# The expert stage of a two-block kernel: weights split by whole units in rings of their own, the further slots' rows on 128 partitions, down products 512 columns wide

## The chip, the cores and the metric

The kernel runs on one core of one Trainium2 chip. The metric is the device time of one execution in microseconds: the median of three runs is 2816.87 us (2815.18 to 2824.26).

## The reference

The program is two transformer blocks on 512 tokens of 1024 features, batch 1, in float32. The first block has two layers, each with a mixer of four kinds (HGRN2, GLA, RWKV7, RetNet, 256 features each) and a feed-forward part; the feed-forward part of its second layer is a mixture of experts. The second block (gated feed-forward, a hybrid of a linear recurrence and windowed attention, gated feed-forward) follows. This case is about the mixture of experts:

```python
def _moe(h, router, wg, wu, wd):            # 8 experts, top 2, hidden width 1408
    probs = jax.nn.softmax((hf @ router).astype(F32), axis=-1)
    top_p, top_i = lax.top_k(probs, TOP_K)
    top_p = top_p / jnp.sum(top_p, -1, keepdims=True)
    gates = jnp.sum(jax.nn.one_hot(top_i, N_EXPERTS, dtype=F32) * top_p[..., None], axis=1)
    for e in range(N_EXPERTS):
        out = out + gates[:, e:e + 1] * _swiglu(hf, wg[e], wu[e], wd[e])
```

`_swiglu(h, wg, wu, wd)` is `(silu(h @ wg) * (h @ wu)) @ wd`.

## The kernel before

**Precision.** A float32 product is made of three products of a rounded type: each operand is split into a high part (an ACT copy, L352) and a low part (a DVE subtraction of the high part, L353), and high x high, high x low and low x high are summed in PSUM. In the expert stage the weights are split on the chip, block by block, as they arrive.

**Routing.** `Moe.route` gives every expert CAP = 160 slots: 128, and CR = 32 further ones. The first expert's inputs are made by products with the slots' places. For the other experts `scatter` writes each token's row to its two slots in DRAM (`xg`) and the gates to `gg`, by indirect DMAs on POOL's queue, while the first expert runs. A token that finds no slot is computed in a branch, `moe_overflow`, at the end of the stage.

**One expert** (`Moe.experts`, once for each of 8) has 33 units of weights, each [128, 1024] float32, 512 KB, loaded on SP's queue:

- gate and up: 11 hidden blocks, each with a gate and an up unit. A unit holds 8 weight blocks of 128 x 128; a block takes two products: high weights against 320 columns (160 slots, high and low part side by side; L1857) and low weights against 160 columns (L1859, the last of a unit L1856). A copy (L1861) and a sum (L1862) take the result from its bank; the silu (L1869), a product of the 32 further slots on POOL (L1871, `rest`) and one of the 128 slots on DVE (L1872) follow, and the hidden rows are split (`hid`).
- down (`moe_down`): 11 units of 128 hidden rows x 1024 columns. The 128 slots are the stationary side; three products in each of four pieces of 256 columns (L2008 to L2010). The 32 further slots are multiplied in plain float32 with the unsplit weights, after every second unit (L2005); the four products of two hidden blocks use four column groups of the array.
- `moe_store` scales the result by the gates and writes it to `yg` in DRAM, on SP's queue.

**Weights.** `Stream` loads a unit into a ring of WR = 3 raw tiles (L661; the down units into a ring of WD = 4), and splits it in four pieces of 256 columns into a ring of WB = 10 pairs of pieces, 2.5 units. A raw tile is free again when its pieces are split and, in down, when L2005 has read it; a piece when its products are done.

**Inputs of the next expert** (`Moe.inputs`). At the last hidden block but one of an expert, SP is asked for the next expert's rows: 128 rows and 32 rows of 1024 columns. After the down blocks in INPUTS (3, 7, 9) PE transposes three, three and two blocks of 128 features, each for both row tiles (L1777); then DVE multiplies by the gain (L1723), POOL adds the bias (L1724), ACT copies the high part (L1725) and POOL subtracts for the low part (L1726).

**Side work.** After each hidden block and each down block, `tick` lets one step of side work go on POOL's queue: scatter in expert 0, clearing in expert 1, the norm's gain and bias on the tokens' rows in expert 2 (eight steps, L1800), the residual's factor in expert 3 (four steps, L1815), gathering the other experts' rows and adding them in expert 7 (L1782, L1826).

**The order of the work.** The order on each engine and queue is fixed when the program is built: a planner goes through the traced instructions in program order, with assumed durations, and lets an instruction go early when its buffers are free. `keep_in_program_order` and `issue_after` pin an instruction behind others of its engine. Queues run strictly in order, SP's too: a load that waits for its buffer holds up what is behind it. The pool of the stage (`me`) waits for all users of the memory that the mixer's pools held before it.

Of the kernel before, what the change touches and what calls it, by code (L numbers as in the profile page):

```python
# [9 lines left out]
F32 = mybir.dt.float32  # L10
# [26 lines left out]
WD = 4  # L37
# [239 lines left out]
def finish(steps):  # L277
    """run a generator, for what it returns"""
# [7 lines left out]
class K:  # L286
# [36 lines left out]
    def warm(self, x, n, bank=None):  # L323
        """keep the tensor engine's clock up over a wait: products of x, at hand, that nothing reads"""
# [37 lines left out]
    def load_x(self, pool, st=None):  # L362
        """the split input, its loads between those of the first weights"""
# [96 lines left out]
    def enter(self, f, hs=slice(0, T)):  # L460
        """block f of the residual, scaled by the next norm's gain: the high part"""
# [17 lines left out]
    def ln_chain(self, tot, sT, g, b, pool, st):  # L479
        """what follows each half of the last output blocks: the norm's input, its statistics, the normed split"""  # L480
# [62 lines left out]
    def resid_in(self, f, sT):  # L543
        """ALPHA times the residual"""
# [68 lines left out]
class Totals:  # L613
    """the Stats' sums per token of the tiles ts, [128 t, len(ts)] each; first() takes what is there before the last blocks"""
# [15 lines left out]
    def first(self):  # L630
        self.add(0)
# [9 lines left out]
class Stream:  # L641
    """the split weights of src, block by block; from unit own on in the pool's own ring"""
# [14 lines left out]
    def load(self, pool=None, bufs=WR):  # L657
        """the next 1024 columns"""
# [31 lines left out]

TWO_PI = 2.0 * math.pi
# [11 lines left out]
INPUTS, PLACES = (3, 7, 9), 9  # L703
# [6 lines left out]
def trig(k, pool):  # L710
    """cosine and sine of the rotary angles, kept in DRAM"""
# [29 lines left out]
class Slots:  # L741
    """a pool whose tiles all share one tag"""
# [1734 lines left out]
```

## Time and profile before

| | |
|---|---|
| median of 3 runs | 2816.87 us (2815.18 to 2824.26) |
| profiled execution, span (first to last instruction) | 2820.5 us |
| mean granted TensorE clock | 0.983 of full speed |
| PE busy | 2716.5 us (96%) |
| DVE busy | 1748.2 us (62%) |
| ACT busy | 1415.1 us (50%) |
| POOL busy | 284.8 us (10%) |
| DMA | 334.07 MB, 118 GB/s on average |
| expert stage, first gate product to last down product | 663.6 us |

PE is the matrix engine's products, PEld its weight loads (they run beside products), DVE, ACT and POOL the vector, scalar and general engines, SP the queue that issues most DMAs. A line such as L353 is a line of the kernel before; L352 and L353 stand for all splits, so the tile names tell which one. Consecutive products overlap in the records, so a product's pitch is read from starts, not from its duration. The granted clock is given as a share of 2.4 GHz.

### The profile page before, as it was taken

How to read it: one execution, taken by the hardware profiler on the slowest of the kernel's cores; microseconds unless marked ns; L12 is line 12 of the kernel's file. 1: busy time of each engine (PE TensorE's matmuls, PEld its weight loads, DVE VectorE, ACT ScalarE, POOL GpSimd, SP SyncE). 2: the span in 40 equal slices, each digit the busy share in tenths (PEclk: the TensorE clock that was granted, in tenths of full speed). 3: DMA queues.
4: the chain of work that ended last, by engine and by line, in shares of the span. 5: the costliest groups of instructions: out<-in, count | busy, mean ns of one | idle time of the engine just before them, and what ended most of it. 6: DMA issues, size and time to landing. Idle time of an engine off the chain costs nothing. (4 is left out here: it accounts for less than half of the span.)

```text
span 2820.5 us, 52447 instructions
## 1 busy us (share of the span) xinstructions
PE 2716.5 (96%) x19484; PEld 2213.6 (78%) x19484; DVE 1748.2 (62%) x4164; ACT 1415.1 (50%) x3561; POOL 284.8 (10%) x362
## 2 busy tenths in 40 slices
PE   8999999999999999998989999889999999999998
PEld 6777688888877776786878888768888877888887
DVE  6664464443476544666998888886554378755543
ACT  5454344333344543465767777664443357544432
POOL 1000120000021000123232111310000010100000
PEclk9999999999999999989999999999999999999999
DMA  4111323322221111168767777733322221232222
GB/s 160 47 46 54 142 67 106 97 98 90 90 85 40 46 61 61 53 221 250 231 224 228 244 249 240 249 99 105 97 97 97 86 74 46 91 99 96 97 96 75
DMA packets 95094, 334.07 MB, mean 118 GB/s; under 512 B 11489, under 2 KB 13953, under 8 KB 94832
## 3 DMA queue, kind: packets, MB, share of 16 engines
q1 hardware_dynamic: 88432, 311.24, 33.7%
q0 software_dynamic: 5824, 18.72, 2.0%
q8 instruction: 156, 2.56, 0.4%
q14 instruction: 106, 0.87, 0.1%
q10 hardware_dynamic: 576, 0.69, 0.1%
HBM read 313.95 MB, written 17.18 MB: 117 GB/s over the span
## 5 line engine op out<-in xcount | busy, mean ns | idle before, releaser
L353 DVE TENSOR_TENSOR wlo<-wraw,whi 128x256 fp32r<-128x256 f32 x2220 | 952.7, 450 | 703.4 <-ACT whi L352 671.4
L352 ACT ACTIVATE whi<-wraw 128x256 fp32r<-128x256 f32 x2220 | 850.2, 411 | 941.6 <-PE bkA L384 760.7
L383 PE MATMUL bkA<-xH,whi 128*128 128x512 f32 x1352 | 542.0, 401 | 2.5 <-DVE sh L916 2.1
L384 PE MATMUL bkA<-xL,whi 128*128 128x512 f32 x1352 | 535.0, 396 | 0.0
L385 PE MATMUL bkA<-xH,wlo 128*128 128x512 f32 x1352 | 533.1, 394 | 0.0
L1857 PE MATMUL bkA<-xe,whi 128*128 128x320 f32 x1408 | 386.2, 351 | 10.9 <-ACT whi L352 10.4
L1859 PE MATMUL bkA<-xe,wlo 128*128 128x160 f32 x1232 | 309.7, 251 | 21.3 <-DVE wlo L353 19.9
L383 PEld LDWEIGHTS bkA<-xH,whi 128*128 128x128 f32 x1352 | 254.9, 189 | 70.8 <-issue 15.2
L384 PEld LDWEIGHTS bkA<-xL,whi 128*128 128x128 f32 x1352 | 255.2, 189 | 59.2 <-issue 10.1
L385 PEld LDWEIGHTS bkA<-xH,wlo 128*128 128x128 f32 x1352 | 255.1, 189 | 56.4 <-issue 4.3
L1857 PEld LDWEIGHTS bkA<-xe,whi 128*128 128x128 f32 x1408 | 262.1, 194 | 15.7 <-ACT whi L352 15.2
L1859 PEld LDWEIGHTS bkA<-xe,wlo 128*128 128x128 f32 x1232 | 241.6, 196 | 40.8 <-DVE wlo L353 38.8
L383 PE MATMUL bkA<-hH,whi 128*128 128x512 f32 (+1 forms) x548 | 207.0, 378 | 0.0
L384 PE MATMUL bkA<-hL,whi 128*128 128x512 f32 (+1 forms) x548 | 206.7, 377 | 0.0
L385 PE MATMUL bkA<-hH,wlo 128*128 128x512 f32 (+1 forms) x548 | 206.5, 377 | 0.0
L385 PEld LDWEIGHTS bkA<-hH,wlo 128*128 128x128 f32 x548 | 102.9, 188 | 21.2
L384 PEld LDWEIGHTS bkA<-hL,whi 128*128 128x128 f32 x548 | 103.0, 188 | 20.9
L383 PEld LDWEIGHTS bkA<-hH,whi 128*128 128x128 f32 x548 | 103.0, 188 | 20.9
L2008 PE MATMUL bkA<-whi,hid 128*128 128x256 f32 x352 | 105.6, 300 | 10.9 <-ACT whi L352 10.9
L2008 PEld LDWEIGHTS bkA<-whi,hid 128*128 128x128 f32 x352 | 67.3, 191 | 52.5 <-ACT whi L352 44.1
L2010 PE MATMUL bkA<-wlo,hid 128*128 128x256 f32 x352 | 100.6, 286 | 3.8 <-DVE wlo L353 3.7
L2009 PE MATMUL bkA<-whi,hid 128*128 128x256 f32 x352 | 99.4, 282 | 0.0
(703 smaller groups left out, 4142.6 us busy)
## 6 DMA issues: line engine op xcount, KB each, us to landing
wraw<-moew SPq DMA_DIRECT2D x264, 512.0 KB, 4.4
wraw<-win SPq DMA_DIRECT2D x76, 512.0 KB, 3.5
wraw<-f0gu SPq DMA_DIRECT2D x44, 512.0 KB, 3.4
wraw<-f1gu SPq DMA_DIRECT2D x44, 512.0 KB, 3.4
wraw<-f2gu SPq DMA_DIRECT2D x44, 512.0 KB, 3.4
wraw<-f0d SPq DMA_DIRECT2D x22, 512.0 KB, 3.5
wraw<-f1d SPq DMA_DIRECT2D x22, 512.0 KB, 3.4
wraw<-f2d SPq DMA_DIRECT2D x22, 512.0 KB, 3.5
```

What stands on the lines that cost most here:

```text
L352: nc.scalar.activation(hi, x, AF.Copy)
L353: nc.vector.tensor_tensor(lo, x, hi.bitcast(F32), op=OP.subtract)
L383: mm(ps, wH, xH, start=first, stop=False)
L384: mm(ps, wH, xL, start=False, stop=False)
L385: mm(ps, wL, xH, start=False, stop=last)
L1857: mm(ps, wH, xf[:, q], start=q == 0, stop=last, skip_group_check=True)
L1859: mm(ps[:, :C], wL, xe[:, q, 0], start=False, stop=False, skip_group_check=True)
L2008: mm(o, hid[:, hb, 0], wH, start=hb == 0 and c * WC % 512 == 0, stop=False, **kw)
L2009: mm(o, hid[:, hb, 1], wH, start=False, stop=False, **kw)
L2010: mm(o, hid[:, hb, 0], wL, start=False, stop=last, **kw)
```

## The change

All in the expert stage:

- A class `MoeStream` replaces `Stream` there. Of every eight units three (`SHARE`) go to the kernel's common ring of 3 raw tiles and five to a ring of MR = 5 of its own; the split parts go to rings of MW = 4 whole units, one ACT copy and one DVE subtraction of 1024 columns each.
- `moe_down` takes the blocks in groups of REST = 4: it fetches and splits the units of the group, then issues the small rows' products of the group, then the products of each block, 512 columns wide.
- `inputs` loads the 32 further rows as four pieces of 256 columns on four times 32 partitions, so all transposes take 128 rows: 4 + 4 for the 128 slots, 2 for the further ones, after blocks 2, 5 and 8. The rows of expert 1 are loaded on POOL's queue, the others on SP's. The four steps behind the transposes (`take_rows`) stay on DVE, POOL, ACT, POOL, for 512, 512 and 256 columns.
- `moe_store` issues on POOL's queue. The side work of experts 2 and 3 is spread over experts 2 to 6, one step in PACE = 8 ticks.
- `hid`, `rest`, `xe`, the row tiles and the store's tiles have one buffer instead of two; the two pools of the stage wait tile by tile for earlier users of their memory. The register load for the overflow branch is placed behind the last weight load on SP.
- Docstrings and comments are dropped.

```diff
-WD = 4
+MR, MW, SHARE = 5, 4, (0, 3, 6)
...
+class MoeStream(Stream):
+    def __init__(self, K_, src, pool):
+        super().__init__(K_, src)
+        self.pool = pool
+    def load(self):
+        k = self.K
+        self.u += 1
+        if self.u % (WR + MR) in SHARE:
+            raw = k.ws.tile([P, 1024], F32, name="wraw", tag="wraw", bufs=WR)
+        else:
+            raw = self.pool.tile([P, 1024], F32, name="mraw", tag="mraw", bufs=MR)
+        self.last = k.nc.sync.dma_start(raw, self.src[self.u])
+        return raw
+    def pieces(self, raw):
+        hi, lo = [self.pool.tile([P, 1024], F32R, name=n, tag=n, bufs=MW) for n in ("mhi", "mlo")]
+        self.K.split(raw, hi, lo)
+        return hi, lo
+    def block(self):
+        if self.j == 8:
+            self.cur, self.j = self.unit(), 0
+        c = slice(self.j * P, self.j * P + P)
+        self.j += 1
+        return [t[:, c] for t in self.cur]
...
-INPUTS, PLACES = (3, 7, 9), 9
+INPUTS, PLACES = (2, 5, 8), 9
+REST, PACE = 4, 8
...
+    def take_rows(self, src, xe, fs, cs, t):
+        nc = self.k.nc
+        g, b = [self.k.par(n)[:, fs] for n in ("ln1g1", "ln1b1")]
+        hi, lo = xe[:, fs, 0, cs], xe[:, fs, 1, cs]
+        n, c = hi.shape[1:]
+        t = t[:, :n * c].rearrange("p (n c) -> p n c", c=c)
...
+            nc.vector.tensor_tensor(t, src, g[:, :, None].to_broadcast([P, n, c]), op=OP.mult)
+        nc.gpsimd.tensor_tensor(t, t, b[:, :, None].to_broadcast([P, n, c]), op=OP.add)
         nc.scalar.activation(hi, t, AF.Copy)
+        return nc.gpsimd.tensor_tensor(lo, t, hi.bitcast(F32), op=OP.subtract)
...
     def inputs(self, e, me):
+        q = nc.gpsimd if e == 1 else nc.sync
+        a, b = me.tile([P, D], F32, name="xra"), me.tile([P, 2 * P], F32, name="xrb")
+        r0 = e * CAP
+        q.dma_start(a, k.xg[r0:r0 + P, :])
+        for n in range(P // CR):
+            q.dma_start(b[n * CR:(n + 1) * CR], k.xg[r0 + P:r0 + CAP, n * 2 * P:(n + 1) * 2 * P])
+        yield
+        xe = me.tile([P, KT, 2, CAP], F32R, name="xe")
         yield xe
+        for src, fs, cs in ((a, slice(0, 4), slice(0, P)), (a, slice(4, KT), slice(0, P)), (b, slice(0, KT), slice(P, CAP))):
+            bank = k.bankB()
+            n = 4 if src is a else 2
+            for f in range(n):
+                c = fs.start * P + f * P
+                nc.tensor.transpose(bank[:, f * P:(f + 1) * P], src[:, c:c + P], k.ident)
...
+            yield self.take_rows(v, xe, fs, cs, me.tile([P, 512], F32, name="ge", tag="ge", bufs=2))
...
-                    yield
+                    yield from range(PACE)
...
-        with tc.tile_pool(name="me", bufs=1) as me:
+        with tc.tile_pool(name="me", bufs=1, reuse_waits="tile") as me, \
+                tc.tile_pool(name="mr", bufs=1, reuse_waits="tile") as mr:
+            ws = MoeStream(k, k.A["moew"], mr)
+            slow = [gains(), residual()]
...
-                        rv = nc.values_load(self.most[0:1, 0:1], min_val=0, max_val=T)
+                        with tc.issue_after(ws.last.ins):
+                            rv = nc.values_load(self.most[0:1, 0:1], min_val=0, max_val=T)
...
+def moe_down(k, ws, hid, rest, side):
+    def fetch():
+        raws.append(ws.raw())
+        cut.append(ws.pieces(raws[-1]))
     for hb in range(NHE):
+        if hb % REST == 0:
+            group = range(hb, min(hb + REST, NHE))
+            for _ in group:
+                fetch()
+            for b in group:
                 for n in range(2):
                     r0 = 32 * (2 * n + b % 2)
                     mm(rb[r0:r0 + CR], rest[:, b], raws[b][:, n * 512:(n + 1) * 512], start=b < 2, stop=b >= NHE - 2, **kw)
+        last = hb == NHE - 1
+        side(hb)
+        wH, wL = cut[hb]
+        for n in range(2):
+            c = slice(n * 512, (n + 1) * 512)
+            mm(yb[n], hid[:, hb, 0], wH[:, c], start=hb == 0, stop=False, **kw)
+            mm(yb[n], hid[:, hb, 1], wH[:, c], start=False, stop=False, **kw)
+            mm(yb[n], hid[:, hb, 0], wL[:, c], start=False, stop=last, **kw)
...
-    nc.sync.dma_start(out[:P], y)
+    nc.gpsimd.dma_start(out[:P], y)
```

## Rows read from the trace of the kernel before

**Rows 1.** The page's first line

```profile
span 2820.5 us, 52447 instructions
```

**Rows 2.** Stretches, per expert: length, busy PE, PEld, DVE, ACT, POOL, clock, DMA, GB/s

```profile
1208.50:1305.70 97.20, 81.69 (x549) 70.14 (x549) 63.19 (x178) 56.98 (x181) 28.77 (x35) 0.91 0.81 242
1305.70:1385.10 79.40, 76.71 (x546) 66.49 (x545) 66.85 (x182) 56.82 (x182) 18.45 (x21) 0.98 0.76 248
1385.10:1470.60 85.50, 75.12 (x547) 66.33 (x546) 81.96 (x183) 57.14 (x183) 29.54 (x25) 0.98 0.67 220
1470.60:1548.80 78.20, 75.91 (x547) 65.22 (x546) 67.73 (x181) 56.12 (x182) 21.45 (x21) 1.00 0.74 241
1548.80:1776.70 227.90, 226.81 (x1635) 195.89 (x1633) 201.95 (x550) 172.24 (x548) 31.66 (x51) 1.00 0.74 243
1776.70:1872.10 95.40, 80.46 (x534) 70.67 (x532) 81.74 (x183) 56.33 (x182) 31.61 (x27) 0.91 0.66 212
```

**Rows 3.** Timeline of PE in gate and up of expert 5 (start, length, line)

```profile
1645.04 0.24 PE L1859 MATMUL bkA<-xe,wlo 128*128 128x160 f32 x1
...
1646.32 0.24 PE L1859 MATMUL bkA<-xe,wlo 128*128 128x160 f32 x1
```

**Rows 4.** Timeline of PE in down of expert 5

```profile
1685.55 0.28 PE L2010 MATMUL bkA<-wlo,hid 128*128 128x256 f32 x1
1685.76 1.07 PE L2005 MATMUL bkB<-wraw,rest 128*32 128x512 f32 x8
1686.76 0.39 PE L2008 MATMUL bkA<-whi,hid 128*128 128x256 f32 x1
...
1687.10 0.28 PE L2010 MATMUL bkA<-wlo,hid 128*128 128x256 f32 x1
...
1689.55 0.28 PE L2010 MATMUL bkA<-wlo,hid 128*128 128x256 f32 x1
1689.66 1.31 PE L1777 MATMUL bkB<-ca,xr 128*128 128x128 f32 x6
1690.91 0.64 PE L2005 MATMUL bkB<-wraw,rest 128*32 128x512 f32 x4
```

**Rows 5.** Waits in the expert stage: total us, times, longest

```profile
PEld bkA L2008 <- ACT whi L352: 44.1, 41, 10.9
...
PEld bkA L1859 <- DVE wlo L353: 38.8, 79, 2.6
```

**Rows 6.** Groups by line, expert stage: busy, mean ns | idle before, releasers

```profile
L353 DVE TENSOR_TENSOR wlo<-wraw,whi 128x256 fp32r<-128x256 f32 x1051 | 467.2, 481 | 82.0 <-ACT whi L352 69.1 <-PE bkA L1859 3.3 <-PE bkA L1857 2.9
...
L352 ACT ACTIVATE whi<-wraw 128x256 fp32r<-128x256 f32 x1053 | 376.0, 406 | 121.1 <-DMA wraw<-moew 87.8 <-PE bkA L1859 10.4 <-PE bkA L1857 7.3
```

**Rows 7.** Stretches: gate scatter, a full one, two with a lower clock

```profile
1264.00:1286.00 22.00, 12.60 (x89) 9.34 (x88) 9.66 (x29) 8.12 (x28) 9.85 (x10) 0.87 1.01 177
1214.00:1218.00 4.00, 4.00 (x33) 4.00 (x32) 2.59 (x9) 3.44 (x12) 0.70 (x2) 1.00 1.03 412
1280.20:1290.40 10.20, 2.94 (x16) 2.71 (x19) 2.51 (x6) 3.37 (x10) 1.49 (x2) 0.50 0.87 244
1396.30:1399.60 3.30, 3.30 (x16) 3.30 (x15) 3.25 (x11) 1.89 (x7) 0.68 (x2) 0.50 0.56 187
```

**Rows 8.** Groups by line and shape: a DVE product 1024 columns wide

```profile
L1301 DVE TENSOR_TENSOR Qp<-Qp,FT 128x1024 f32<-128x1024 f32 x6 | 7.3, 1218 | 2.6 <-ACT FT L1266 2.6
```

**Rows 9.** Timeline of PE before the stage: products of 512 columns

```profile
1167.39 0.39 PE L383 MATMUL bkA<-yH,whi 128*128 128x512 f32 x1
...
1168.79 0.39 PE L383 MATMUL bkA<-yH,whi 128*128 128x512 f32 x1
```

**Rows 10.** Timeline of PE in the routing: 128-row transposes

```profile
1182.38 0.60 PE L1587 MATMUL bkA<-ca,ZR 128*128 128x128 f32 x4
```

**Rows 11.** Timeline of POOL and DVE in expert 2

```profile
1405.18 2.43 POOL L1800 TENSOR_TENSOR hTok<-hTok,lnrow 128x1024 f32<-128x1024 f32 x1
1405.29 2.60 DVE L353 TENSOR_TENSOR wlo<-wraw,whi 128x256 fp32r<-128x256 f32 x1
```

More of the change, by code (lines that the diff above doesn't have):

```diff
@@ L1687, in route @@
                            start=n == 0 and i == 0 and q == 0, stop=i == NT - 1 and q == 1, skip_group_check=True)
-            self.take(b, self.xe0, fs, self.sl.tile([P, 3, C], name="ge"), True)
+            self.take(b, self.xe0, fs, self.sl.tile([P, 3, C], name="ge"))
         V.tensor_reduce(mx, gate, axis=AX.X, op=OP.add)
@@ L1708, in route, with take @@
         V.tensor_copy(self.most, mb[:, P - 1:P])
-    def take(self, bank, xe, fs, t, first=False):
+    def take(self, bank, xe, fs, t):
         nc = self.k.nc
-        V = nc.vector
         f, n = fs[0], len(fs)
@@ L1815, in residual @@
                 nc.gpsimd.tensor_scalar(h[:, i], h[:, i], ALPHA, None, op0=OP.mult)
-                yield
+                yield from range(PACE)
         def collect():
@@ L1835, in places @@
             return cp
-        with tc.tile_pool(name="me", bufs=1) as me:
+        with tc.tile_pool(name="me", bufs=1, reuse_waits="tile") as me, \
+                tc.tile_pool(name="mr", bufs=1, reuse_waits="tile") as mr:
+            ws = MoeStream(k, k.A["moew"], mr)
             nxt = self.xe0
+            slow = [gains(), residual()]
             for e in range(NE):
                 xe = nxt
-                beside = [self.scatter(), self.slot_gates(me)] if e == 0 else [clear()] if e == 1 else [gains()] if e == 2 else [residual()] if e == 3 else [collect()] if e == NE - 1 else []
+                beside = [self.scatter(), self.slot_gates(me)] if e == 0 else [clear()] if e == 1 else [collect()] if e == NE - 1 else slow
                 def tick(after):
@@ L1863, in hidden @@
                     return a
-                hid = me.tile([P, NHE, 2, P], F32R, name="hid", tag="hid", bufs=2)
-                rest = me.tile([P, NHE, CR], F32, name="rest", tag="rest", bufs=2)
+                hid = me.tile([P, NHE, 2, P], F32R, name="hid")
+                rest = me.tile([P, NHE, CR], F32, name="rest")
                 for hb in range(NHE):
@@ L1876, in experts @@
                         step = self.inputs(e + 1, me)
-                        nxt = next(step)
+                        next(step)
+                if e + 1 < NE:
+                    nxt = next(step)
                 def side(hb):
@@ L1890, in experts @@
                 at, after = [], [last]
-                yb, rb = moe_down(k, ws, hid, rest, me, side)
+                yb, rb = moe_down(k, ws, hid, rest, side)
                 gs = [self.gs[:, n, e:e + 1] for n in range(2)]
@@ L1985, in combine @@
                 scale(i - 2)
-def moe_down(k, ws, hid, rest, pool, side):
+def moe_down(k, ws, hid, rest, side):
     nc = k.nc
@@ L1994, in moe_down @@
     kw = dict(skip_group_check=True)
-    raws = []
+    raws, cut = [], []
+    def fetch():
+        raws.append(ws.raw())
+        cut.append(ws.pieces(raws[-1]))
     for hb in range(NHE):
-        raws.append(ws.raw(pool, WD))
-        last = hb == NHE - 1
-        pieces = ws.pieces(raws[hb])
-        side(hb)
-        if hb % 2 or last:
-            for b in range(hb - hb % 2, hb + 1):
+        if hb % REST == 0:
[3 more added lines that the diff above has]
+            for b in group:
                 for n in range(2):
@@ L2005, in moe_down @@
                     mm(rb[r0:r0 + CR], rest[:, b], raws[b][:, n * 512:(n + 1) * 512], start=b < 2, stop=b >= NHE - 2, **kw)
-        for c, (wH, wL) in enumerate(pieces):
-            o = yb[c * WC // 512][:, c * WC % 512:c * WC % 512 + WC]
-            mm(o, hid[:, hb, 0], wH, start=hb == 0 and c * WC % 512 == 0, stop=False, **kw)
-            mm(o, hid[:, hb, 1], wH, start=False, stop=False, **kw)
-            mm(o, hid[:, hb, 0], wL, start=False, stop=last, **kw)
+        last = hb == NHE - 1
[6 more added lines that the diff above has]
+            mm(yb[n], hid[:, hb, 0], wL[:, c], start=False, stop=last, **kw)
     return yb, rb
@@ L2015, in moe_store @@
     nc = k.nc
-    y = pool.tile([P, D], F32, name="yr", tag="yr", bufs=2)
-    r = pool.tile([P, 512], F32, name="yq", tag="yq", bufs=2)
+    y = pool.tile([P, D], F32, name="yr")
+    r = pool.tile([P, 512], F32, name="yq")
     for n in range(2):
```

33 lines of the change are left out of this document (10 added, 23 removed).

## The prediction

> **What bounds the kernel now.** I read the page first: the span is 2820.5 us [rows 1]; the median of the three runs shown, 2816.87, lies 3.6 us (0.13%) under this one execution. All sums are made against the span, and the saving is then taken off the median as it is. A difference of 0.3% (8.5 us) is about what a measurement of this kernel can tell from none.
>
> The second view is the table of stretches, cut at the first gate product of each expert [rows 2]. The stage takes 663.6 us: experts 4 to 6 together 227.9 (75.97 each), expert 1 79.4, expert 2 85.5, expert 3 78.2, the first 97.2 and the last 95.4. The reader should see that PE is busy nearly all the time in experts 4 to 6, that DVE is busy 201.95 of 227.9 there (67.3 per expert), and 81.96 of 85.5 in expert 2.
>
> PE's busy time hides its waits because products overlap, so the third view gives the pitch. In gate and up, from one L1859 product to the fifth after it is 1.28 us: 0.256 per block [rows 3]. An expert has 22 units of 8 blocks: 176 x 0.256 = 45.06 us. In down, 21 products of 256 columns take 2.45 us: 0.1167 each, 132 of them 15.40. The group of small-row products (8 records, two hidden blocks) puts 1.21 us between two down products that stand 0.117 apart otherwise, so it costs 1.09; six make 6.54. Six transposes take 1.25, sixteen 3.33 [rows 4]. Sum 70.3. A steady expert thus loses 75.97 - 70.3 = 5.6 us to waits, the others more.
>
> What PE waits for is the split of the weights: 44.1 us for ACT's high part in down, 38.8 for DVE's low part in gate and up [rows 5]; behind it, ACT stood 87.8 us for the weights' DMAs and DVE 69.1 for ACT [rows 6]. So the stage is PE at full pitch plus a run-ahead too short to cover late weights (3 raw units, 2.5 split ones) and stretches where DVE is held up.
>
> **The change, part by part.** *Deeper rings.* Raw units in flight go from 3 (4 in down) to 8, split ones from 2.5 to 4. At 2.05 us a unit the raw ring covers 16 us. The DMA must bring 33 units of 0.524 MB and about 1.3 MB of rows and results in 68 us: 274 GB/s, where the stage now moves 243 [rows 2] and a 4 us stretch moved 412 [rows 7]. The price of more transfers in flight is unseen: between 0 and the 5.6 us that the waits cost now.
>
> *Splits in whole units.* DVE's 256-column subtraction lasts 0.481, ACT's copy 0.406 [rows 6]. A 1024-column DVE product of two tensors lasts 1.218 [rows 8]; four of the small ones 1.92, with overlapping records. For DVE I take 0.2 us saved per unit, 6.6 per expert (bounds 0, and 33 x 0.70 = 23). ACT's 1024 columns stand nowhere: between one 0.406 and four, 1.62; I take 1.0. Against it, the first block of a unit waits for 1.0 + 1.22 = 2.2 us of splitting instead of 0.89. With three units split ahead (6.1 us in gate and up, 4.2 in down) that is covered; with none ahead it is 2.2 at each place where PE arrives first.
>
> *Products 512 wide.* Six 512-column products start in 1.40 us: 0.2333 each [rows 9]. 66 of them take 15.40, exactly the 132 of before: nothing gained, nothing lost.
>
> *Small rows in groups of four blocks.* Three groups instead of six, 16 records instead of 8. The second eight cost at most the 1.00 us from the first record to the next down product; so a group costs 1.09 to 2.09, I take 2.0, three make 6.0: 0.5 saved (0.3 to 3.3). Each group needs four raw units landed at once; the ring holds eight.
>
> *Inputs.* Ten 128-row transposes replace sixteen. Four back to back last 0.60 [rows 10], at most 0.15 each, less with overlap: I take 0.12, and 0.3 for entering and leaving: 1.5, or 1.8 saved per expert (1.5 to 2.1). POOL's adds and subtractions keep their 2560 columns. The last of the three chains (now at block 8, not 9) must end before the next gate product, and it holds 32 slots of every feature, so the first product needs it. Three down units, 4.2 us, lie behind its transposes; its four instructions and their waits come to 3 to 7 us. I take 0.5 late per expert (0 to 2.8).
>
> DVE's subtraction that starts 0.11 us after POOL's 2.43 us add lasts 2.60 and not 0.48, one side of a lock [rows 11]. The Trainium skill (page "SBUF — State Buffer", section "Who interferes with whom") says that the two exclude each other for the whole instruction, whichever issues first. By that rule POOL's add and subtraction may each wait up to 1.22 us instead of 0.48 behind a whole-unit subtraction: 1.5 us per expert, 10 us over seven, and the sum below would be 2747; no run here shows that side with a wide instruction.
>
> *POOL's side work.* The eight gains and four residual scalings (about 2.45 us each) now stand 8 ticks apart, 22 ticks to an expert: 2.75 per expert over experts 2 to 6. Before, eight made expert 2 9.5 us slower than a steady one and four made expert 3 2.2 slower: 1.2 and 0.55 each. Alone, with three units ahead, I take 0.25 each: 0.7 per expert (0 to 3.3).
>
> *Queues.* Result stores and the second expert's rows move from SP to POOL, so no weight load stands behind their waits; three more plain issues per expert on POOL, which is busy 10.5 us of 76, are hidden. If POOL falls behind, only rest products and row chains wait. SP issues four row pieces instead of one; it has 2 us per unit. The register load for the overflow branch goes behind the last weight load; its value is long there, so nothing changes at the end. Single buffers for hid, rest, xe and the stores are rewritten at least a hidden block (4.1 us) after their last reader, so I cost them at nothing; if that cover fails, one wait of about 2 us per expert.
>
> **The sum.** A plain expert at pitch: 45.06 + 15.40 + 6.0 + 1.5 = 68.0. I leave 1.5 us of split waits (0 to 5.6), 0.5 for the inputs and 0.7 for POOL: 70.7 for experts 1 to 6, 424.2 in all.
>
> The first: 97.2 contains a wait of 10.9 for ACT's copy [rows 5]. There the gate scatter slows all transfers to 177 GB/s for 22 us [rows 7]; PE at pitch eats 256, so 1.7 MB, 3.3 units, are missing, which eight can cover if full. But the new rings lie on memory of the routing, so only part is loaded ahead: about 4 us at the start (0 to 5), 5 for the second expert's rows behind the scatter (0 to 12), and 3 for clock: the granted clock stood at 0.50, the lower of its two levels (1.2 GHz), for 10.2 us in and after that wait [rows 7]. 68 + 12 = 80.
>
> The last has eight gathers and twelve POOL adds. Its DVE load is 81.74 [rows 2]; less 6.6 it is 75, over PE's 66.5 (no transposes), so DVE sets it: 75 + 4 = 79.
>
> Sum 424.2 + 80 + 79 = 583.2 instead of 663.6: 80.4 saved, span 2740; off the median, **2737 us**.
>
> **The rivals.** *Half of the waits stay* (the order on DVE and ACT, fixed when the program is built, or DVE, which at 60 us plus 6.7 of POOL's lock is nearly as loaded as PE). For it: expert 2 took its DVE load plus 3.5 us. Against: DVE's load falls below PE's. Steady 73.8, first 88, last 86: 617, 2770 us.
>
> *All waits go*: the eight at pitch and 3 us for clock, 547 us, 2700. For it: 412 GB/s and three split units ahead. Against: the last expert's DVE load.
>
> *Slower: the whole-unit split becomes the wait.* If the fixed order starts a group's splits only when PE has arrived, PE stands 2.2 us at the 24 group starts and the 8 expert starts, and each such wait may put the clock at 0.50 for 3.3 us, as a stretch in expert 2 has it [rows 7], 1.7 us more. 32 x 3.9 = 125: 2737 + 125 = 2862. It decides from 21 such places (80 / 3.9). Against it: four split buffers let ACT and DVE work while PE does the group before.
>
> *The change doesn't do what it says*: raw slots are freed only by DVE and by the group's products, so eight slots may still run as three; with the transposes alone gained, 7 x 2.3 = 16 us, and the wider splits costing the same: no change.
>
> **How the numbers follow.** Forecast 0.57 (own range 2718 to 2758, from the first and last experts and 1.5 +- 1.5 of waits); half stay 0.20; all go 0.15; no change 0.03; slower 0.05. Faster 0.57 + 0.20 + 0.15 = 0.92. The range for 8 in 10 reaches from 2705, near the all-go case, to 2778, past the half case: about 0.08 lie below and 0.12 above.
>
> **What would show it.** Right: experts 4 to 6 at 69 to 72 us each, ACT's wait for the weights' DMAs under 20 us in all, no PE wait over 2 us outside the first expert, DVE's unit subtraction at 1.2 us, down products 0.233 apart, three small-row groups of about 2 us, three transpose groups of under 0.6. Wrong: a wait for ACT or DVE before each small-row group (the slower case), clock under 0.95 in the middle experts, or DVE busy over 68 us per expert (half stay). The forecast fails altogether if the plan puts splits behind the inputs' chain, or if transfers with eight in flight land in more than 16 us.

## The result and the profile after

The changed kernel takes 2741.87 us (median of four runs, 2737.01 to 2746.0); the kernel before, in the runs beside it, 2819.64. The ratio is 0.9694, with a 95% interval of 0.9666 to 0.9722. The forecast was 2737, own range 2718 to 2758. The profiled execution has a span of 2744.2 us, 76.3 below that of before; the forecast had 80.4. The sum came out nearly right, but from terms that did not: the first view shows it. It is the table of stretches, one per expert (4 to 6 together), with the columns of [rows 2].

```profile
1211.70:1298.40 86.70, 76.05 (x475) 64.68 (x476) 56.70 (x85) 49.05 (x85) 39.81 (x41) 0.90 0.87 270
1298.40:1366.00 67.60, 67.60 (x473) 59.77 (x472) 54.47 (x83) 46.32 (x83) 21.78 (x24) 1.00 0.81 276
1366.00:1434.10 68.10, 67.92 (x473) 59.60 (x471) 60.57 (x83) 46.68 (x83) 22.35 (x23) 1.00 0.81 275
1434.10:1503.40 69.30, 68.01 (x473) 59.75 (x473) 62.06 (x83) 47.28 (x84) 21.83 (x24) 1.00 0.81 278
1503.40:1706.60 203.20, 203.20 (x1416) 179.43 (x1417) 174.67 (x250) 142.48 (x251) 58.51 (x67) 1.00 0.79 271
1706.60:1784.90 78.30, 71.94 (x467) 61.56 (x465) 74.40 (x91) 46.53 (x89) 39.84 (x29) 0.96 0.75 261
```

Experts 4 to 6 take 67.7 us each: the pitch, as the waits below show. (PE's busy time alone would not: before, it was 226.81 of 227.9 us there [rows 2], with 5.6 us per expert lost.) Experts 1 to 6 together take 408.2 us where 424.2 were forecast. The first takes 86.7 (forecast 80), the last 78.3 (79). The stage is 573.2 us instead of 663.6: 90.4 saved. But 14.1 come back outside it: 3.2 ahead of the stage and 10.9 behind it (959.3 us from 1784.9 to the end against 948.4 from 1872.1), 9.3 of them in one stretch. It is shown next, first in the kernel before, then in the changed one: from the last down product to the first product behind the norm, and in the changed one the part at the low clock.

```profile
1872.30:1892.10 19.80, 16.70 (x76) 10.33 (x75) 13.59 (x48) 14.34 (x33) 1.20 (x1) 1.00 0.18 56
```

```profile
1784.90:1814.00 29.10, 25.61 (x75) 14.73 (x74) 12.04 (x42) 13.46 (x30) 1.20 (x1) 0.65 0.01 2
1789.30:1809.80 20.50, 20.50 (x42) 10.63 (x41) 9.74 (x38) 9.28 (x23) 1.20 (x1) 0.50 0.00 0
```

The work is the same (76 and 75 products), the granted clock is not: 0.50 (1.2 GHz) for 20.5 us, with PE busy all of them.

The waits of PE in the stage (engine, what it stood at, for whom: us, times, longest), first the two largest before, then all of the changed kernel:

```profile
PE bkA L1859 <- DVE wlo L353: 19.9, 17, 2.4
PE bkA L2008 <- ACT whi L352: 10.9, 2, 10.7
```

```profile
PE bkB L1799 <- DMA gslot<-gg: 6.8, 1, 6.8
PE bkA L2067 <- DVE mlo L353: 4.3, 3, 2.0
PE bkA L1906 <- DVE mlo L353: 3.3, 4, 1.8
PE bkA L2065 <- ACT mhi L352: 2.4, 1, 2.4
PE bkA L1904 <- ACT mhi L352: 2.2, 1, 2.2
PE bkA L1904 <- POOL xe L1767: 1.5, 2, 1.3
```

All but the last lie in the first and the last expert; the last is at the starts of experts 3 and 4. The rows of [rows 5], 44.1 and 38.8 us, are of PEld, and a weight load can stand while earlier products still run. Like against like: PEld rows of the changed kernel for weight splits hold at most 6.2 us. In experts 4 to 6 PEld had these two before, and none for a weight split after:

```profile
PEld bkA L2008 <- ACT whi L352: 12.6, 15, 0.8
PEld bkA L1859 <- DVE wlo L353: 8.3, 34, 0.6
```

The splits by line (busy, mean ns of one | idle before), which answer to [rows 6]. They are of the 165 units from the new ring; the 99 from the common one have rows of their own. The 87.8 us for which ACT stood there for weights are gone in both:

```profile
L353 DVE TENSOR_TENSOR mlo<-mraw,mhi 128x1024 fp32r<-128x1024 f32 x165 | 232.9, 1413 | 45.0 <-ACT mhi L352 42.9 <-PE bkB L2059 1.1 <-issue 0.5
L352 ACT ACTIVATE mhi<-mraw 128x1024 fp32r<-128x1024 f32 x165 | 173.2, 1052 | 18.5 <-PE bkA L2066 14.6 <-issue 3.5 <-ACT mhi L352 0.3
```

In down of expert 4 (start, length, line) a group of small-row products stands between a down product and the next one:

```profile
1556.59 0.40 PE L2067 MATMUL bkA<-mlo,hid 128*128 128x512 f32 x1
1556.91 0.62 PE L2059 MATMUL bkB<-wraw,rest 128*32 128x512 f32 x2
...
1558.77 0.50 PE L2065 MATMUL bkA<-mhi,hid 128*128 128x512 f32 x1
```

2.18 us apart, less a pitch of 0.23: the group costs 1.95 (2.0 was taken). Gate and up take 45.1 us (45.06), down 22.3 from its first small-row product, and 0.3 lie between.

### The profile page after: what moved, and what is told of

The parts are those of the page before. It is cut to its first block, busy times and chain, and to the rows that moved or that the text cites. A ratio compares the mean times of both kernels' runs of the same rounds, so it can differ in the third digit from the quotient of the medians.

```text
span 2744.2 us, 48736 instructions
## 1 busy us (share of the span) xinstructions
PE 2661.5 (97%) x18914; PEld 2166.6 (79%) x18914; DVE 1665.4 (61%) x3372; ACT 1335.9 (49%) x2769; POOL 328.1 (12%) x388
## 5 line engine op out<-in xcount | busy, mean ns | idle before, releaser
L352 ACT ACTIVATE whi<-wraw 128x256 fp32r<-128x256 f32 x1164 | 473.5, 415 | 811.8 <-PE bkA L384 751.1
L353 DVE TENSOR_TENSOR wlo<-wraw,whi 128x256 fp32r<-128x256 f32 x1164 | 483.9, 424 | 619.9 <-ACT whi L352 601.5
L1904 PE MATMUL bkA<-xe,mhi 128*128 128x320 f32 x1408 | 365.1, 345 | 3.7 <-ACT mhi L352 2.2
L384 PEld LDWEIGHTS bkA<-xL,whi 128*128 128x128 f32 x1352 | 254.7, 188 | 58.2 <-issue 9.6
L1906 PE MATMUL bkA<-xe,mlo 128*128 128x160 f32 x1232 | 292.3, 237 | 3.3 <-DVE mlo L353 3.3
L353 DVE TENSOR_TENSOR mlo<-mraw,mhi 128x1024 fp32r<-128x1024 f32 x165 | 232.9, 1413 | 45.0 <-ACT mhi L352 42.9
L1904 PEld LDWEIGHTS bkA<-xe,mhi 128*128 128x128 f32 x1408 | 254.8, 191 | 5.0 <-ACT mhi L352 2.5
L1906 PEld LDWEIGHTS bkA<-xe,mlo 128*128 128x128 f32 x1232 | 237.5, 193 | 4.7 <-DVE mlo L353 4.5
L352 ACT ACTIVATE mhi<-mraw 128x1024 fp32r<-128x1024 f32 x165 | 173.2, 1052 | 18.5 <-PE bkA L2066 14.6
L353 DVE TENSOR_TENSOR mlo<-wraw,mhi 128x1024 fp32r<-128x1024 f32 x99 | 131.4, 1327 | 33.8 <-ACT mhi L352 31.3
L352 ACT ACTIVATE mhi<-wraw 128x1024 fp32r<-128x1024 f32 x99 | 104.5, 1056 | 13.0 <-PE bkA L2066 7.7
```

What stands on the lines that cost most here:

```text
L352: nc.scalar.activation(hi, x, AF.Copy)
L353: nc.vector.tensor_tensor(lo, x, hi.bitcast(F32), op=OP.subtract)
L384: mm(ps, wH, xL, start=False, stop=False)
L1904: mm(ps, wH, xf[:, q], start=q == 0, stop=last, skip_group_check=True)
L1906: mm(ps[:, :C], wL, xe[:, q, 0], start=False, stop=False, skip_group_check=True)
```

## The experiments

Every expert's time, from its first gate product to that of the next, and the time from the start of the last down product to the end (the column of expert 7 ends 0.3 us later); then the median and the ratio to the runs of the kernel before beside it.

| kernel | 0 | 1 | 2 | 3 | 4 | 5 | 6 | 7 | to end | median us | ratio (95%) |
|---|---|---|---|---|---|---|---|---|---|---|---|
| before | 97.2 | 79.4 | 85.5 | 78.2 | 76.5 | 75.5 | 76.0 | 95.6 | 948.3 | 2819.64 | |
| changed | 86.7 | 67.7 | 68.1 | 69.2 | 67.8 | 67.7 | 67.7 | 78.3 | 959.5 | 2741.87 | 0.9694 (0.9666 to 0.9722) |
| narrow | 83.9 | 67.7 | 73.3 | 74.3 | 73.3 | 71.0 | 67.8 | 83.2 | 959.6 | 2766.85 | 0.9785 (0.9745 to 0.9826) |
| rest2 | 84.4 | 68.7 | 68.8 | 70.3 | 68.8 | 68.9 | 68.8 | 79.7 | 949.8 | 2736.55 | 0.9699 (0.9646 to 0.9751) |
| raw4 | 85.1 | 69.0 | 69.9 | 70.0 | 69.5 | 69.9 | 69.9 | 82.1 | 961.5 | 2756.3 | 0.9761 (0.9715 to 0.9807) |
| split2 | 96.5 | 76.0 | 83.5 | 82.2 | 82.3 | 77.2 | 76.4 | 85.6 | 963.6 | 2832.62 | 1.0034 (1.0011 to 1.0057) |
| bsplit4 | 94.7 | 81.7 | 88.0 | 78.6 | 79.0 | 79.3 | 79.8 | 94.8 | 957.9 | 2838.37 | 1.0068 (1.0051 to 1.0085) |
| gates | 84.6 | 67.7 | 68.1 | 69.2 | 67.8 | 67.7 | 67.7 | 78.2 | 957.9 | 2733.97 | 0.9694 (0.967 to 0.9719) |
| adds | 85.3 | 67.7 | 68.1 | 69.2 | 67.8 | 67.7 | 67.7 | 111.5 | 951.8 | 2761.32 | 0.9801 (0.9777 to 0.9826) |
| first | 91.7 | 67.7 | 68.1 | 69.2 | 67.8 | 67.7 | 67.7 | 78.3 | 958.5 | 2744.24 | 0.9733 (0.9703 to 0.9762) |
| narrow_raw4 | 82.2 | 70.0 | 73.2 | 76.0 | 73.3 | 71.7 | 71.1 | 90.1 | 950.2 | 2768.45 | 0.9804 (0.9766 to 0.9842) |
| pace1_spq | 80.9 | 67.7 | 79.5 | 67.8 | 67.7 | 67.7 | 67.7 | 78.3 | 947.4 | 2735.28 | 0.9697 (0.9663 to 0.9732) |
| warm3 | 89.6 | 67.7 | 68.1 | 69.3 | 67.8 | 67.7 | 67.7 | 78.3 | 949.5 | 2731.11 | 0.9671 (0.9636 to 0.9706) |
| best | 86.5 | 67.7 | 68.1 | 69.3 | 67.8 | 67.7 | 67.7 | 67.1 | 950.4 | 2723.77 | 0.9655 (0.9626 to 0.9684) |

Where two kernels share an expert's work, experts 1 to 6 agree to 0.1 us. The totals don't repeat so well, since the last column has two values, about 950 and about 960. So mechanisms are judged by experts.

**narrow: four splits of 256 columns.**

```diff
-        self.K.split(raw, hi, lo)
+        for c in range(0, 1024, WC):
+            s = slice(c, c + WC)
+            self.K.split(raw[:, s], hi[:, s], lo[:, s])
```

> The changed kernel with one part undone: each unit is split by four ACT copies and four DVE subtractions of 256 columns into the same rings. In the changed kernel experts 1 to 6 take 67.7 to 69.2 us each, the pitch of the products, so the waits of 5.6 us per expert are gone. Theory of depth (the waits went because more raw and split units run ahead): four pieces start 0.336 us apart on DVE instead of one in 1.15, 0.2 us more per unit, 6.6 us more of DVE per expert, still under PE's 67.7, so experts 1 to 6 stay at 67.7 to 69 and the time within 5 us of the changed kernel's 2742. Theory of width (the waits went because wide instructions leave DVE and ACT more room): 72 to 76 us per expert, 2770 to 2790.

Both theories got a part. Expert 1, without side work on POOL, and expert 6, with one step near its start, stay at 67.7 and 67.8; experts 2 to 5, with two or three steps each, take 71 to 74.3. PE's waits in experts 1 to 6 are not for weights:

```profile
PE bkA L1906 <- POOL xe L1769: 10.1, 4, 3.1
PE bkA L2069 <- DVE mlo L353: 2.8, 3, 1.3
```

DVE is busy 197.58 us in experts 4 to 6 instead of 174.67, the chain that makes the next expert's inputs (DVE, POOL, ACT, POOL) ends later, and the first gate product waits up to 3.1 us for POOL's last subtraction. At three of the four such waits the granted clock is at 0.50 for 3.4 to 6.8 us, 13.6 in all. The waits of the fence (12.9 us) and half of the time at 0.50 (6.8) come to about what experts 2 to 5 lose against the changed kernel (19.1). So beside POOL's side work the width keeps the inputs on time.

**rest2, raw4, split2: groups of two, and on them a raw ring of 4 or a split ring of 2.**

```diff
-REST, PACE = 4, 8
+REST, PACE = 2, 8
```

raw4, and then split2, change one line more:

```diff
-MR, MW, SHARE = 5, 4, (0, 3, 6)
+MR, MW, SHARE = 1, 4, (0, 1, 2)
```

```diff
-MR, MW, SHARE = 5, 4, (0, 3, 6)
+MR, MW, SHARE = 5, 2, (0, 3, 6)
```

> The changed kernel with groups of two hidden blocks in down (REST 2 instead of 4), the rings unchanged. Six groups of small-row products at 1.09 us each instead of three at 1.87 (their measured cost in the changed kernel): 0.9 us more per expert, 68.6 each, 7 us more in all, 2749. The rival, that fetching and splitting four units at once is what keeps down free of waits: split waits of 0.5 to 1 us before each group, 71 to 74 us per expert, 2768 to 2790. It is also the base for the next two, which can't be built with groups of four.

> As the one before (groups of two), with a raw ring of 4 units in all (3 common, 1 own) instead of 8; the split ring stays at 4 units. If the raw ring's depth removed the waits: ACT stands for the weights' DMAs again, experts 1 to 6 at 72 to 76 us, 25 to 45 us above the run with groups of two. If the split ring's depth did: 68 to 70 us each, within 8 us of the run with groups of two. The first expert, where the gate scatter slows the transfers, should be 4 to 10 us longer under either.

> As the run with groups of two, with a split ring of 2 units instead of 4; the raw ring stays at 8. If the split ring's depth removed the waits: PE waits for ACT's and DVE's parts again, experts 1 to 6 at 72 to 78 us. If the raw ring's depth did: 68 to 70 us each, since a unit of split work (1.0 ACT, 1.15 DVE) is shorter than the 2.05 us that PE takes for a unit.

Groups of two cost 1.0 us per expert, as expected from the count of groups (0.9). Between rest2 and raw4, experts 4 to 6 differ by 0.7 to 1.1 us, though ACT stands for weights again; between rest2 and split2, by 7.6 to 13.5, though no weight is late. The first fence has ACT's rows in experts 4 to 6 of raw4, the second a row of PE's weight loads in those of split2.

```profile
ACT mhi L352 <- DMA wraw<-moew: 16.9, 15, 4.7
ACT mhi L352 <- DMA mraw<-moew: 8.1, 8, 2.9
```

```profile
PEld bkA L1906 <- DVE mlo L353: 24.4, 49, 2.1
```

With two whole units one is in use while the other is made, and making it (1.05 us on ACT, then 1.23 on DVE, 2.28 in a row) outlasts the 2.05 us in which PE uses one up. Whole-unit splits thus need more than two units; four were enough, three were not tried. The wait that the slower rival put at 2.2 us exists where they are missing, with a longest of 2.1 us and a mean of 0.5.

**bsplit4: the deeper split ring alone, on the kernel before.** Line numbers move; six of every sixteen pieces lie in the stage's pool (`wx`), and `hid` has one buffer here, too.

```diff
-        if self.pool and self.units > self.own:
+        self.n = getattr(self, 'n', 0) + 1
+        if self.pool and (self.n % 16 >= 10 if self.bufs == 6 else self.units > self.own):
...
+            ws.pool, ws.bufs, ws.n = me, 6, 0
...
-                hid = me.tile([P, NHE, 2, P], F32R, name="hid", tag="hid", bufs=2)
+                hid = me.tile([P, NHE, 2, P], F32R, name="hid")
```

> The kernel before with one thing of the change alone: a split ring of 16 pieces, 4 units, instead of 10 (the six more lie in the stage's pool; hid has one buffer to make room). Raw ring of 3 (4 in down), splits of 256 columns, inputs, queues and side work stay as before. If the split ring's depth is what removed the waits: experts 4 to 6 fall from 76.0 to between 70.3 (their pitch) and 72 us each, expert 2, where eight gains lock DVE, from 85.5 to 76 to 82; 25 to 45 us off the kernel before. If wide splits or the raw ring are needed as well: 74 to 76 each, less than 12 us off.

Neither: it is slower than the kernel before, 79.0 to 79.8 in experts 4 to 6. The rows are PE's and ACT's waits over the whole stage.

```profile
PE bkA L1859 <- DVE mg L1864: 38.1, 38, 3.0
...
ACT whi L352 <- DMA wraw<-moew: 78.6, 73, 9.4
ACT wx L352 <- DMA wraw<-moew: 27.2, 23, 3.6
```

PE's waits for splits fall from 44.9 us in all to 16.9, but it now waits for DVE's sum, which empties its bank. ACT stands 105.8 us for weights (87.8 before). With more pieces ahead of the sums in the fixed order of ACT and DVE, a late weight holds up the sums behind it; that this order is the cause I read from the rows and did not test by itself, nor the single `hid` buffer. In this run a deeper split ring without weights that have landed was worth less than nothing.

**narrow_raw4: narrow splits and the raw ring of 4 together.** Its edits are those of narrow, rest2 and raw4.

> The changed kernel with two parts undone together: splits of 256 columns and a raw ring of 4 (groups of two, split ring of 4 units). Each alone cost little where nothing disturbed: the narrow splits left experts 1 and 6 at 67.7 us, the raw ring of 4 put experts 4 to 6 at 69.5 to 69.9, 1 us over the run with groups of two. Theory that the waits need both, late weights and a DVE too busy to catch up (about 64 of 68 us with narrow splits, against 57): well over the sum of the two, experts 4 to 6 at 73 to 80 and the total at 2785 to 2825. Rival, that the two add up: 70 to 73 for experts 1 and 6, 2770 to 2785.

About additive: experts 1, 5 and 6 take 70.0 to 71.7, experts 2 to 4 73.2 to 76.0. Experts 1 to 6 take 435.3 us in all, where raw4 plus what narrow adds to the changed kernel makes 437.4; single experts lie up to 1.9 below or 1.1 above. So narrow splits and a shallow raw ring don't explain the 76 of before between them. What is left (a raw ring of 3 in gate and up, 2.5 split units, the old inputs, stores on SP, products of 256 columns) was not taken apart further.

**pace1_spq: side work at one step a tick, stores and the second expert's rows on SP.**

```diff
-REST, PACE = 4, 8
+REST, PACE = 4, 1
...
-        q = nc.gpsimd if e == 1 else nc.sync
+        q = nc.sync
...
-    nc.gpsimd.dma_start(out[:P], y)
+    nc.sync.dma_start(out[:P], y)
     for n in range(2):
-        nc.gpsimd.dma_start(out[P:, n * 512:(n + 1) * 512], r[64 * n:64 * n + CR])
+        nc.sync.dma_start(out[P:, n * 512:(n + 1) * 512], r[64 * n:64 * n + CR])
```

> The changed kernel with two parts undone that different experts show: the side work of experts 2 and 3 at one step a tick (the eight gains and four residual scalings all in expert 2), and the result stores and the second expert's rows on SP's queue. Experts 4 to 6 show the queue: 67.7 if eight raw units cover the stores' waits, 69 to 72 if the queue's order was what made weights late. Expert 2 shows the side work: twelve locks of 2.4 us in a row; 68 to 70 if the rings cover them, as the spread ones are covered; 74 to 80 if spreading is what removed the 9.5 us that expert 2 lost before.

Expert 2 takes 79.5, experts 4 to 6 67.7. Its stretch, then experts 4 to 6:

```profile
1352.90:1432.30 79.40, 71.45 (x473) 60.02 (x471) 74.48 (x83) 45.72 (x82) 51.98 (x29) 1.00 0.69 234
1500.10:1703.30 203.20, 203.20 (x1418) 179.38 (x1417) 167.76 (x250) 141.54 (x250) 36.63 (x51) 1.00 0.77 274
```

Twelve locks in one expert raise DVE from 55.9 us (167.76 / 3) to 74.48, over PE's 67.7, and the rings of eight and four units don't cover that: spreading the side work is a part of its own, worth 11.4 us in expert 2 at a price of 1.4 in expert 3. The queue of the stores is worth nothing in experts 4 to 6. The first expert, at 80.9, is the shortest of all. That could mean that the second expert's rows were better off on SP, but it is one trace, and narrow_raw4, with these rows on POOL, has 82.2: not shown.

**gates: gate scatters right behind their rows.**

```diff
-        for out, src, done in ((self.k.xg, lambda w, i: self.hTok[:, i], rows),
-                               (self.k.gg, lambda w, i: self.gts[w][:, i:i + 1], gates)):
-            for w, ii in enumerate(self.idx):
-                for i in range(NT):
+        for w, ii in enumerate(self.idx):
+            for i in range(NT):
+                for out, src, done in ((self.k.xg, self.hTok[:, i], rows), (self.k.gg, self.gts[w][:, i:i + 1], gates)):
...
-                    if done is rows or i == NT - 1:
-                        yield
+                yield
```

> The changed kernel with another order of the scatter in expert 0: each row scatter is followed by its gate scatter, in the hidden blocks 1 to 8, instead of all eight gate scatters at the end of gate and up and in down. In the changed kernel POOL stands 7.84 us for the gate scatters to land, behind it ACT 8.71 us for POOL's add of the next inputs, and PE 6.84 us for the slots' gates. If that order is the cause, the landing has passed by then: expert 0 falls from 86.7 to 74 to 80 us, the total by 7 to 13. The rival, that the gate scatters slow the weights wherever they stand: expert 0 stays within 3 us, with new waits for weights in gate and up.

The rival. In the changed kernel the fence below is the end of the first expert: POOL stands for the gate scatters, ACT behind POOL, PE for the slots' gates.

```profile
1286.60 0.60 POOL L1793 DMA_DIRECT2D gslot<-gg  x1 [7.84 <-DMA gg<-gg,ii]
...
1288.96 0.63 ACT L1766 ACTIVATE xe<-ge 128x512 fp32r<-128x512 f32 x1 [8.71 <-POOL ge L1765]
...
1293.16 0.24 PE L1799 MATMUL bkB<-ca,gslot 8*128 8x8 f32 x1 [6.84 <-DMA gslot<-gg]
```

ACT had stood 7.89 us for POOL's add once before, until 1276.79: there POOL was still issuing the eight scatters (1262.37 to 1275.47). With the scatters moved, the waits of the fence go, but POOL stands 17.33 us for the scattered rows, and the weights come late: 199 GB/s from 1237 to 1247 us of gates, where the changed kernel has 389 from 1240 to 1250, and ACT stands 14.5 us for weights. 84.6 us against 85.3 to 89.6 in the four traces with the old order (changed, adds, warm3, best) is no clear gain.

**adds: the last expert's additions on DVE.**

```diff
-                    nc.gpsimd.tensor_tensor(acc[:, i], acc[:, i], (h if w == 0 else y)[:, i], op=OP.add)
+                    V.tensor_tensor(acc[:, i], acc[:, i], (h if w == 0 else y)[:, i], op=OP.add)
```

> The changed kernel with the eight additions of the last expert (the residual and the second slot's rows) on DVE instead of POOL. On POOL each lasts 2.4 us, and DVE's subtraction beside it 4.06 instead of 1.21; on DVE each should last 1.21, as other 1024-column operations do. If POOL's lock sets the last expert: from 78.3 to 68 to 73 us. The rival, that DVE's own load or the gathers that it then waits for set it: 77 or more. For the clock after the stage (0.50 for 20.5 us in the changed kernel's trace, about 10 us lost): if it falls because of PE's stalls in the last expert it stays at full speed here; if because of the 2.5 us at the branch it falls as before.

111.5 us: DVE stood 41.7 us at additions whose rows had not landed, and PE 26.3 us for the splits that DVE made behind them.

```profile
DVE x L1870 <- DMA x<-yg,ii: 22.8, 4, 7.5
DVE x L1870 <- DMA yv<-yg,ii: 18.9, 4, 5.0
```

The clock stayed up after the stage. That doesn't clear PE's stands in the last expert: here they all end by 1780.8 us, 27 us ahead of the last down product, while in the changed kernel two lie in down. In warm3, below, PE stands in the last expert no less than in the changed kernel, and the clock stays up: these stands alone don't lower it.

**first: the first two units through the common ring.**

```diff
+        self.units += 1
+        if self.units <= 2:
+            return [self.piece(raw[:, c:c + WC]) for c in range(0, 1024, WC)]
...
```

> The changed kernel with the stage's first two units split into the common ring of small pieces, as all units were before, instead of the new rings. In the changed kernel the first product waits 2.19 us for ACT's copy and the second 0.63 for DVE, though eight raw units have landed 37 us earlier, since the new split tiles lie on memory of the routing or stand behind its work on ACT. If that is the cause the wait at the start goes: 2.8 us, and with an earlier end of the low clock up to 6. If the copies come late only by the order on ACT: no change within 1 us at the start.

Neither. The first wait is 1.54 us instead of 2.19, but each further piece is made late too (three waits of 0.51, one of 1.68 for ACT), gate and up of the first expert take 55.9 us instead of 49.3, and the low clock lasts longer. In both kernels ACT's first copy of a weight follows at once on its last copy of the first expert's inputs (L1750, L1755), though ACT had stood idle 1.54 us shortly before: the copies came late by their place on ACT, not only by memory.

**warm3 and best: products ahead of the branch, and the additions on DVE two blocks later.** best is warm3 with the second edit added. In both, the register load and the branch are asked for behind the down products, not inside the last block; `self.dve` is DVE's product of the hidden block, in down the last split asked for.

```diff
-                    if e + 1 == NE and hb == NHE - 1:
...
+                    with tc.issue_after(ws.mm.ins):
+                        for _ in range(3):
+                            pin(mm(wb, h[:, 0, :P], h[:, 0, :512], start=True, stop=True))
...
+                    with tc.If(rv > LIM):
...
-            for n in range(3 * NT):
+            for n in range(3 * NT + 2):
...
+                m = n - NT - 2
+                if m >= 0:
+                    with tc.issue_after(self.dve.ins):
+                        V.tensor_tensor(acc[:, m % NT], acc[:, m % NT], (y if m >= NT else h)[:, m % NT], op=OP.add)
```

> The changed kernel with three products in plain float32 (128 x 512, results unused) behind the last down product, ahead of the branch to the overflow. In ten traces so far the clock falls to 0.50 for 20 us after the stage where PE stood 2.1 to 4.8 us at that branch, and stays at full speed where it stood 1.3 to 2.08. If that stand sets the clock: PE stands under 1 us, the clock stays up, the stretch from the last down product to the first product behind the norm falls from 29 to 20 us, the total by 8 to 10. If the branch only starts later by as much, the same 2.5 us stand stays and nothing is gained, or 3 us lost.

> The run with three products ahead of the branch, and with the last expert's eight additions on DVE, each two hidden blocks later than in the run that had them on DVE too early, where DVE stood 41.7 us for the gathers. If the gathers have landed by then, each addition costs DVE 1.21 us instead of holding it for 2.4: the last expert falls from 78.3 to 69 to 73 us, and with the clock kept up behind it the total to 2720 to 2730. The rival, that gathers land later still or DVE is full with its own work: 77 us or more for the last expert.

Both held, and best's last expert came out shorter than the range it was given. In warm3 the products take 2.74 us, PE then stands 0.30 instead of 2.48, and the stretch behind the stage is 20.2 us at full clock, though PE stood 7.9 us in the last expert, 6.3 in the changed kernel. On PE's queue the branch ends 2.4 us behind the last down product, 2.2 in the changed kernel; so its new place is not what shortens the stand, the products fill it:

```profile
1781.03 2.74 PE L1944 MATMUL bkA<-hTok 128*128 128x512 f32 x6
1784.07 1.15 PE L1985 MATMUL bkB<-last 128*128 128x512 f32 x4 [0.30 <-PEq L1947]
```

```profile
1781.30:1801.50 20.20, 19.07 (x80) 11.07 (x78) 11.71 (x41) 15.18 (x31) 1.20 (x1) 1.00 0.01 3
```

Its four runs (2724.92 to 2733.73, mean granted clock 0.985 to 0.988) lie below all four of the changed kernel (2737.01 to 2746.0, 0.981 to 0.985), but the ratios' intervals overlap: the totals alone would not decide. In best the last expert takes 67.1 us, PE busy in all of it, with DVE at 63.58 instead of 74.40:

```profile
1705.10:1772.20 67.10, 67.10 (x468) 59.23 (x467) 63.58 (x99) 47.55 (x89) 18.97 (x21) 1.00 0.81 300
```

best has the lowest median of all: 2723.77 us (2718.14 to 2732.97, six runs). Its ratio's interval still touches that of the changed kernel, but no run of the one reaches a run of the other.

## Why the prediction was right, and where it was not

That the stage would run near PE's pitch was right. That the total came within 5 us of the forecast is luck: experts 1 to 6 were 16.0 us better, the first expert 6.7 and the time outside the stage 14.1 worse. Of the signs that it named, two did not hold: experts 4 to 6 came out under the 69 to 72 us, and one PE wait in the last expert is 2.03 us, over the 2 allowed.

- **Pitch, right.** 68.0 was worked out, 67.7 measured: gate and up 45.1, groups of small rows 1.95, products 512 wide 0.23 apart, so next to nothing gained or lost by their width. The ten transposes, with what they put between products, cost about 1.1 (1.5 taken).
- **"I leave 1.5 us of split waits", 0.5 for the inputs, 0.7 for POOL: mis-sized.** They measure 0 in experts 1 and 4 to 6, 0.4 and 1.5 in experts 2 and 3. For experts 1 to 6 the rival in which all waits go (chance 0.15) was the right one, 16.0 us below the forecast. Nor did the 10 us come that would have made the sum 2747: the lock does hold POOL off, as the last section shows, but the inputs were late at two expert starts only, 1.5 us in all.
- **The cause of the waits, shown in part.** "A run-ahead too short" holds for the raw ring by about 1 us (raw4), though the prediction gave it the first place. For the split ring, split2 shows that whole-unit splits need more than two units; it doesn't show that the 2.5 units of pieces before were too few, and four of them on the kernel before gained nothing (bsplit4). Apart from split2 no run that undoes a part brings back 5.6 us in an expert without side work, so which parts removed them stays open. For the steady experts the 44.1 us in down [rows 5] were also misread: expert 5 before spent 26.0 us in down, 0.7 over its pitch, and 49.4 in gate and up, 4.3 over. DVE's 43.32 us there nearly fill the pitch of 45.1, which its mean over an expert hides. The rows are gate and up of a steady expert: before, changed, narrow (columns of [rows 2]).

```profile
1625.30:1674.70 49.40, 49.16 (x354) 46.34 (x353) 43.32 (x127) 38.73 (x127) 3.40 (x10) 1.00 0.80 260
1571.20:1616.60 45.40, 45.40 (x353) 45.24 (x352) 40.39 (x67) 33.79 (x67) 9.90 (x15) 1.00 0.81 277
1657.10:1702.60 45.50, 45.45 (x352) 45.37 (x352) 44.84 (x138) 40.47 (x139) 8.08 (x14) 1.00 0.82 274
```

- **DVE's load, 6.6 us less: more came off.** In experts 4 to 6 it falls from 67.3 us each to 58.2, or to 55.9 in pace1_spq, where they hold no side work, as before; the width's share is 7.6 (narrow). With the new rings DVE can be busy 44.84 of 45.50 us and PE keeps its pitch; what fails first is the inputs' punctuality (narrow).
- **POOL's side work, right.** Spread locks are covered, bundled ones cost 11.4 us in expert 2 (twelve there; before, eight and four).
- **Queues at nothing: right for the stores, open for the second expert's rows.**
- **The first expert, 80 against 86.7.** The prediction covered the missing weights with eight raw units. They were, but the gate scatter has two more readers: POOL's queue, behind which the next inputs stand, and the slots' gates. That "if POOL falls behind, only rest products and row chains wait" was the failed step: ACT waits for the row chain (7.89 and 8.71 us), and the splits stand behind ACT. Gate and up took 4.1 us more than in a steady expert, about what was given to the start; down took 14.8 more, where 5 stood for the rows.
- **The last, 79 against 78.3: right, for the reason given,** DVE's load (75 taken, 74.40 measured); take eight locks out of it and 67.1 are left, near the 66.5 of PE's pitch (best). The prediction counts twelve adds on POOL; both kernels have eight.
- **Outside the stage, 0 against 14.1: missed.** One edit reaches there, the register load behind the last weight load, of which the prediction said that "nothing changes at the end". The branch that reads it lasts 5.26 us on PE's queue instead of 3.46, partly beside products queued ahead of it, and PE stands 2.48 instead of 2.08; no run takes that edit back, so its share is not shown. Start of the stage: the profiled executions begin it anywhere from 1201.1 to 1213.7 us, so 3.2 is their scatter. Behind it: -16.0 + 6.7 - 0.7 + 14.1 = 4.1, the distance from the forecast's span of 2740.1 to 2744.2.

What sets the clock behind the stage is not settled. Of fourteen traces six have it at full speed where PE stood 0.3 to 2.08 us at the branch, seven at 0.50 where it stood 2.08 (bsplit4, with 0.60 more right behind it) to 4.8, and one, pace1_spq, at full speed after 2.90. The four stands of 0.30 to 1.77 us were all followed by the full clock, of the ten of 2.05 to 4.81 three; the length alone doesn't decide. Five of the twelve traces without the three products kept the clock, so two traces with them are a good sign and no proof.

## What to carry to other kernels

A deeper ring need not pay by itself: four units of split pieces gained nothing on the kernel before, while with whole-unit splits two units cost 7.6 to 13.5 us per expert. Where making a part outlasts using one (2.28 against 2.05 us here), two are too few. Compare the load of the engine that prepares operands with PE's pitch phase by phase, not as a mean, and spread or move whatever locks it. After a gain, look at the stretch behind the changed one: here a tenth of it was lost there to the clock, and in both traces with three idle products it was not.

## What the runs showed of the hardware

The lock between POOL and DVE has two sides, and the prediction had seen one. These rows are of the last expert of the changed kernel.

```profile
1753.53 3.38 POOL L1870 TENSOR_TENSOR x<-x,yv 128x1024 f32<-128x1024 f32 x1
...
1753.37 1.27 DVE L353 TENSOR_TENSOR mlo<-mraw,mhi 128x1024 fp32r<-128x1024 f32 x1
1754.57 2.48 DVE L353 TENSOR_TENSOR hid<-mg,hid 128x128 fp32r<-128x128 f32 x1
```

POOL's addition, 2.40 us when alone, starts 0.16 us after DVE's wide subtraction and lasts 3.38; DVE's next, small one (0.28 alone) then lasts 2.48. That agrees with the rule of the Trainium skill (page "SBUF — State Buffer", section "Who interferes with whom") that the one which comes first holds the other off for its whole instruction. Another row doesn't fit it so plainly: DVE's subtraction that started at 1736.51 lasted 4.06 us beside a POOL addition recorded from 1737.09 to 1739.49, 0.58 us after it. POOL's spans are rough, so this stays open.

At a data-dependent branch that is not taken PE stood 1.3 to 4.8 us, unless further products were queued ahead of it (0.30 and 0.54 us); on PE's queue it lasted 3.46 to 5.80 us over the fourteen traces. While the eight scatters of 128 gates, four bytes each, were on their way (POOL's wait for them ends at 1286.60 us), the DMA engines were as busy as ever (share 1.03 from 1280 to 1290 us, 1.04 from 1240 to 1250) and moved 147 GB/s instead of 389.
